# Weight blocks of half the size, more buffers of half the size, and conditioning products eight at a time

## The chip, the cores and the metric

The kernel runs on one core of a Trainium2 chip. The metric is the time of one execution on the device, in microseconds (us), as the median of three runs. A profiled execution is taken beside them.

## The reference, cut to what matters

It is one inference step of a two-layer decoder trunk, all in float32, for 256 prompt tokens and 8 sequences of 4 new tokens each (288 columns of work in all).

```python
cond = silu(c)
for layer in range(2):
    mod = cond @ w_ada[layer] + b_ada[layer]            # (2048) x (2048, 12288)
    sh1, sc1, g1, sh2, sc2, g2 = split(mod, 6)
    h = rms(x, g_mix[layer]) * (1 + sc1) + sh1
    y = mixer(h)            # layer 0: GLA + gated DeltaNet; layer 1: SSD + S5
    x = x + g1 * y
    h = rms(x, g_ffn[layer]) * (1 + sc2) + sh2
    up = causal_dwconv(h @ w_up[layer])                 # (2048) x (2048, 11264)
    a, g = split(up, 2)
    x = x + g2 * ((silu(g) * a) @ w_down[layer])        # (5632) x (5632, 2048)
y = rms(x, g_final)
```

Each mixer has an input projection (`w_in_ab`, `w_in_cd`), recurrences in chunks with many small products, and an output projection.

## The kernel before, in words

**Weights and products.** Every large matrix goes through `weights` (line 170): a block of 4 tiles of 128 input rows by 256 output columns is loaded from HBM by SyncE's DMA queue into a buffer `raw` (512 KB, pool `wraw`, 5 buffers), ScalarE rounds it to `whi` (line 179), VectorE takes the remainder `wlo = raw - whi` (line 180), both into pool `whl` (3 buffers each), and TensorE makes 24 products of 288 columns with it (lines 206 to 208 in `project`, 235 to 237 in `project_parts`, which runs the first projection): high times high, high times low, low times high, for each of 4 tiles and 2 halves of the columns.

**Conditioning.** The modulation vectors `mod` of both layers need 12 matrices of 2048 by 2048 that are used once, with 9 columns of data padded to 32. Here the weight is what streams: `ada_groups` (line 1912) makes four products of 512 columns with a stationary `cond` of 32 columns, one on each quarter of the array's columns. `ada_quarter` (line 1945) does the first two matrices in pieces at the start; `ada_steps` (line 1918) does the ten later ones as background work: it loads one tile of 128 rows in two DMAs of 512 KB, makes its four products, and so on 16 times. These loads (`araw`) share the 5 buffers of `wraw`.

**Pace.** `weights` calls `c.step()` (line 57) for each block; a step advances the generators that `c.background` has registered, one `yield` each so many steps. The tables of S5 and the conditioning for layer 1 run so behind the first feed-forward.

**Order.** The program is written in one sequence; a scheduler then sets the order on each engine by priority (program order) and by its own estimate of what is ready, and gives out the buffers. Each engine runs its order strictly. A product may so be moved between others, but a queue never overtakes itself. Waits are by semaphores; the loads of SyncE and ScalarE share eight of them (`DMAHW0` to `DMAHW7`), and a load waits until the earlier one on its semaphore has landed.

**Small loads.** `rows_in` (line 447) brings convolution states in through a `raw` buffer, `RB` = 6 columns of tiles at a time; `load_consts` (line 670) brings in constants in pieces of 1024 columns. `small_proj` (line 1970) uses the same pools.

**Stages by time in the profile.** 0 to 246 us: start, conditioning of the first mixer, `project_parts`. 246 to 984 us: first mixer and its output projection. 984 to 1804 us: feed-forward of layer 0. 1804 to 2460 us: second mixer. 2460 to 3279 us: feed-forward of layer 1, with conditioning in its first part only.

Of the kernel before, what the change touches and what calls it, by code (L numbers as in the profile page):

```python
# [9 lines left out]
F32 = mybir.dt.float32  # L10
# [5 lines left out]
P = 128  # L16
# [3 lines left out]
T = SEQ + NS * DS  # L20
TS = T + NS + 2
D = 2048
KT = D // P
FF = 5632
EPS = 1e-6
RB = 6
# [15 lines left out]


class Ctx:
    raw_bufs, hl_bufs, kb = 5, 3, 4
    count = 0

    def __init__(self):
# [170 lines left out]
def project_parts(c, w, cols, act, part, tick, ready):  # L219


    nc = c.nc
    for q in range(KT // 4):
        for i, (c0, out, scale) in enumerate(cols):
            tick(q, i)
            if i == part and q + 1 < KT // 4:
                ready(q + 1)
            hi, lo = weights(c, w, 4 * q, 4, c0, 2 * P)
            ps = c.pp.tile([P, 2, 512], F32, tag="pp", name="pp")
            for j in range(2):  # L230
                js = slice(j * P, (j + 1) * P)
                for k in range(4):
                    ah, al = act(4 * q + k)
                    o = ps[:, j, :T]
                    nc.tensor.matmul(o, hi[:, k, js], ah, start=(k == 0), stop=False)  # L235
                    nc.tensor.matmul(o, hi[:, k, js], al, start=False, stop=False)  # L236
                    nc.tensor.matmul(o, lo[:, k, js], ah, start=False, stop=(k == 3))  # L237
            if q == 0:
                nc.scalar.activation(out, ps[:, :, :T], AF.Copy, scale=scale)
            else:  # L240
                nc.vector.scalar_tensor_tensor(out, ps[:, :, :T], scale, out, ALU.mult, ALU.add)
# [202 lines left out]
    return [(st[i * rows:(i + 1) * rows], d[i]) for i in range(q)]  # L444


def rows_in(c, o, src, rows, nt, q, stage=None, RB=RB):

    nc = c.nc
    m = nt // q  # L450
    ov = o.rearrange("p (c q) r -> p c (q r)", q=q)
    w = q * rows
    g = 512 // w
    stage = stage or (lambda: c.wraw.tile([P, RB * P], F32, tag="raw", name="rowst"))
    parts = []
    for s0 in range(0, m, RB):
        sn = min(RB, m - s0)
        st = stage()[:, :RB * P].rearrange("p (c n) -> p c n", n=P)
        parts.append((s0, sn, st))
        for a, b in row_parts(st[:w, :sn], src, s0, sn, rows, q):  # L460
            nc.gpsimd.dma_start(a, b)

    def place():
        for s0, sn, st in parts:
            for c0 in range(0, sn, g):
                n = min(g, sn - c0)
                ps = mtile(c)
                for j in range(n):
                    transpose(c, ps[:, j * w:(j + 1) * w], st[:w, c0 + j, :])
                nc.scalar.copy(ov[:, s0 + c0:s0 + c0 + n, :], ps[:, :n * w].rearrange("p (c w) -> p c w", w=w))  # L470

    return place
# [197 lines left out]
def load_consts(c, cf, cm):  # L670
    nc = c.nc
    c.seg = c.const.tile([P, 13, P], F32R, name="seg")
    m8 = c.const.tile([P, NCM], mybir.dt.uint8, name="cm8")
    for dst, src, n in ((c.seg.rearrange("p l t -> p (l t)"), cf, 13 * P), (m8, cm, NCM)):
        for o in range(0, n, 1024):
            m = min(1024, n - o)
            st = c.wraw.tile([P, 1024], F32, tag="raw", name="craw")
            nc.sync.dma_start(st[:, :m], src[:, o:o + m])
            nc.vector.tensor_copy(dst[:, o:o + m], st[:, :m])
    c.pre, c.suf = c.seg[:, 7, :].bitcast(F32), c.seg[:, 8, :].bitcast(F32)  # L680
    c.segs = c.seg[:, 9:13, :]
    c.pres, c.sufs = c.seg[:, 11, :].bitcast(F32), c.seg[:, 12, :].bitcast(F32)
    c.sel = c.const.tile([P, 64], F32R, name="sel")
    nc.vector.tensor_copy(c.sel, c.cf[:, NS + 35:NS + 99])
    c.mk = m8[:, :8 * P].rearrange("p (l t) -> p l t", t=P)
    c.mkT = m8[:, 8 * P:15 * P].rearrange("p (l t) -> p l t", t=P)
# [1225 lines left out]
def ada_groups(c, ps, cond, pieces, ks, first, last):  # L1912

    for r in range(4):
        c.nc.tensor.matmul(ps[32 * r:32 * r + 32, :], cond[:, ks[r], :], pieces[r], start=first, stop=last)  # L1915


def ada_steps(c, cond, w, which, bias, mod):

    nc = c.nc  # L1920
    ps = c.pa.tile([P, 512], F32, tag="pa", name="pa")
    for k in range(KT):
        pieces = []
        for h in range(2):
            raw = c.wraw.tile([P, 1024], F32, tag="raw", name="araw")
            nc.sync.dma_start(raw, w[k * P:(k + 1) * P, which * D + h * 1024:which * D + (h + 1) * 1024])
            pieces += [raw[:, 0:512], raw[:, 512:1024]]
            if h:
                ada_groups(c, ps, cond, pieces, [k] * 4, k == 0, k == KT - 1)
            yield  # L1930
    pt = mtile(c)
    for t in range(0, 4, 2):
        sb = c.misc.tile([P, T], F32, tag="tmp", name="adas", bufs=2)[:, :2 * P]
        nc.scalar.copy(sb, ps[:, t * P:(t + 2) * P])
        for j in range(2):
            transpose(c, pt[:, (t + j) * P:(t + j + 1) * P], sb[:, j * P:(j + 1) * P])
    pv = pt.rearrange("p (t j s) -> p j t s", t=4, j=4)
    mv = mod.rearrange("p (j t) s -> p j t s", t=4)
    bv = bias.rearrange("p (j t) -> p j t", t=4)
    for t in range(4):  # L1940
        nc.vector.tensor_tensor(mv[:, :, t], pv[:, :, t, 0:9], bc(bv[:, :, t], 2, 9), ALU.add)
    yield


def ada_quarter(c, cond, w, which, q, bias, mod):

    nc = c.nc
    ps = c.pa.tile([P, 512], F32, tag="pa", name="pa")
    c0 = which * D + q * 512
    for k in range(0, KT, 4):  # L1950
        pieces = []
        for k0 in (k, k + 2):
            raw = c.wraw.tile([P, 2, 512], F32, tag="raw", name="araw")
            nc.sync.dma_start(raw, w[k0 * P:(k0 + 2) * P, c0:c0 + 512].rearrange("(k p) n -> p k n", p=P))
            pieces += [raw[:, 0], raw[:, 1]]
            if k0 > k:
                ada_groups(c, ps, cond, pieces, range(k, k + 4), k == 0, k == KT - 4)
            yield
# [303 lines left out]
def trunk(tc, I, O):  # L2262
    nc = tc.nc
    with ExitStack() as ctx:
# [107 lines left out]
        fso = lambda l: O["ffn_conv_s"][l].rearrange("s j n -> (s j) n")  # L2372
        with tc.tile_pool(name="s5prep", bufs=1, reuse_waits="tile") as tp:
            c.background(1.9, *[ada(l, i) for l, i in ((0, 5), (1, 1), (1, 0), (1, 2))])
            c.background(2, s5_tables(c, tp, I["s5_A_re"][0], I["s5_A_im"][0], I["s5_log_dt"][0],
                                      (I["s5_B_re"][0], I["s5_B_im"][0]), (I["s5_C_re"][0], I["s5_C_im"][0]), s5d))
            c.pace(math.inf)
            c.pace(1.5, 48)
            ss1, h1 = SumSquares(c, x), norm("g_mix1", 1, 1, 0)
            ffn(c, 0, x, h, ss, mods[0][:, 5], pr, I["w_ffn_up"][0], I["w_ffn_down"][0], fst(0), O["ffn_conv_p"][0, 0], fso(0),  # L2380
                done(ss1, h1))
            c.finish()
# [75 lines left out]
```

## Time and profile before

| | us |
|---|---|
| median of 3 runs | 3285.08 |
| lowest and highest | 3272.85, 3291.9 |
| profiled execution, its own time | 3281.18 |
| its span from first to last instruction | 3279.2 |
| granted TensorE clock, mean | 0.99 |
| TensorE (PE) busy | 3178.5 (97%) |
| VectorE (DVE), ScalarE (ACT) busy | 2074.9 (63%), 1456.5 (44%) |
| moved by DMA | 663.82 MB, mean 202 GB/s |

Products on PE overlap: one is shown as some 0.3 us long, while the next starts 0.13 us after it. So a full PE is read from how many products start in a stretch and from the distance of their starts, not from the busy share. PEld are the weight loads of PE. A conditioning product stands in the trace as two records. A line is that of the kernel's file before, unless it is said otherwise.

### The profile page before, as it was taken

Reading aid. Unit: us, or ns where it says so; the run is one execution under the profiler, and the core shown is the slowest. Engines: PE = TensorE matmul, PEld = TensorE weight load, DVE = VectorE, ACT = ScalarE, POOL = GpSimd, SP = SyncE. Lnnn points to the kernel's source line nnn. Section 1 sums busy time; section 2 is a strip of 40 time slices with the busy share of each in tenths; the row PEclk is TensorE's granted clock in tenths of the full one; section 3 lists DMA queues with packets and bytes.
Section 4 is the critical chain, followed back from the end, with each engine's and each line's share of the span. In section 5 each row is a group of like instructions: output and inputs, shape, how many; then the busy total and the mean of one; then the engine's idle time right before and its main releaser. Section 6 shows DMA issues by size and latency. Waiting matters only on the chain.

```text
span 3279.2 us, 58982 instructions
## 1 busy us (share of the span) xinstructions
PE 3178.5 (97%) x23220; PEld 2839.6 (87%) x23220; DVE 2074.9 (63%) x4303; ACT 1456.5 (44%) x2286; POOL 430.4 (13%) x792
## 2 busy tenths in 40 slices
PE   7999999999999999999999999999999999999998
PEld 3678777888989999999999977877989999999997
DVE  3346756666787566667665776667775556565566
ACT  2333333343554434343444675444464435444353
POOL 2010011111231100010101210112131001010020
PEclk9999999999999999999999999999999999999999
DMA  8876675455667777778777665764467755555553
GB/s 292 264 224 193 200 253 154 152 172 173 184 208 233 225 234 242 236 239 254 234 242 233 201 199 169 242 211 158 150 198 229 226 167 167 163 165 168 166 172 108
DMA packets 506617, 663.82 MB, mean 202 GB/s; under 512 B 42409, under 2 KB 436454, under 8 KB 506330
## 3 DMA queue, kind: packets, MB, share of 16 engines
q1 hardware_dynamic: 470930, 610.68, 58.8%
q0 software_dynamic: 14272, 40.76, 4.1%
q10 hardware_dynamic: 21136, 8.61, 1.0%
q8 instruction: 183, 3.00, 0.4%
q14 instruction: 96, 0.78, 0.1%
HBM read 634.13 MB, written 25.79 MB: 201 GB/s over the span
## 4 chain that ended last, share of the span: by engine, by line
PE 83%; DMA 8%; ACT 3%; DVE 3%; issue 2%; POOL 0%; SPq 0%; ACTq 0%; DVEq 0%; POOLq 0%
PE pp L206 22%; PE pp L208 21%; PE pp L207 21%; PE pa L1915 6%; DMA raw<-in_w_in_ab 2%; DMA raw<-in_w_in_cd 2%; PE pm L121 1%; DMA araw<-in_w_ada 1%; DVE wlo L180 1%; ACT whi L179 1%; PE pp L237 1%; PE pp L235 1%; PE pm L1125 1%; PE pp L236 1%; PE pm L1121 1%
## 5 line engine op out<-in xcount | busy, mean ns | idle before, releaser
L180 DVE TENSOR_TENSOR wlo<-raw,whi 128x1024 fp32r<-128x1024 f32 x768 | 944.4, 1231 | 736.4 <-ACT whi L179 725.0
L179 ACT CAST whi<-raw 128x1024 fp32r<-128x1024 f32 x768 | 805.4, 1049 | 1278.9 <-PE pp L207 671.4
L206 PE MATMUL pp<-hhi,whi 128*128 128x288 f32 (+1 forms) x4480 | 1347.9, 301 | 3.2 <-ACT whi L179 1.9
L208 PE MATMUL pp<-hhi,wlo 128*128 128x288 f32 (+1 forms) x4480 | 1339.1, 299 | 6.8 <-DVE wlo L180 6.6
L207 PE MATMUL pp<-hlo,whi 128*128 128x288 f32 (+1 forms) x4480 | 1336.2, 298 | 0.1
L206 PEld LDWEIGHTS pp<-hhi,whi 128*128 128x128 f32 x4480 | 848.9, 190 | 121.2 <-issue 81.5
L208 PEld LDWEIGHTS pp<-hhi,wlo 128*128 128x128 f32 x4480 | 848.5, 189 | 23.6 <-DVE wlo L180 11.3
L207 PEld LDWEIGHTS pp<-hlo,whi 128*128 128x128 f32 x4480 | 848.4, 189 | 11.0 <-issue 9.8
L206 PE MATMUL pp<-hh,whi 128*128 128x288 f32 x1408 | 417.3, 296 | 0.0
L208 PE MATMUL pp<-hh,wlo 128*128 128x288 f32 x1408 | 416.6, 296 | 0.0
L207 PE MATMUL pp<-hl,whi 128*128 128x288 f32 x1408 | 413.5, 294 | 0.0
L1915 PE MATMUL pa<-araw,cond 128*32 128x512 f32 x1536 | 265.8, 606 | 12.5 <-DMA araw<-in_w_ada 12.2
L206 PEld LDWEIGHTS pp<-hh,whi 128*128 128x128 f32 x1408 | 264.7, 188 | 15.1 <-issue 13.4
L207 PEld LDWEIGHTS pp<-hl,whi 128*128 128x128 f32 x1408 | 266.6, 189 | 0.0
L208 PEld LDWEIGHTS pp<-hh,wlo 128*128 128x128 f32 x1408 | 264.2, 188 | 0.1
L532 DVE SCALAR_TENSOR_TENSOR cv<-pad,params,cv 128x304 f32<-128x304 f32 (+1 forms) x460 | 224.8, 533 | 20.3 <-ACT cv L530 12.0
L525 POOL COPY ffnpo<-pad 128x4 f32<-128x4 f32 x88 | 66.9, 761 | 1223.0 <-ACT pad L522 1223.0
L431 DVE SCALAR_TENSOR_TENSOR x<-pp,mod,x 128x256 f32<-128x256 f32 x256 | 112.4, 479 | 76.7 <-PE pp L208 75.8
L530 ACT ACTIVATE cv<-pad,params 128x304 f32<-128x304 f32 (+1 forms) x212 | 125.3, 637 | 8.9 <-ACT pad L523 1.1
L1915 PEld LDWEIGHTS pa<-araw,cond 128*32 128x32 f32 x1536 | 39.3, 108 | 63.5 <-issue 35.4
L235 PE MATMUL pp<-hhi,whi 128*128 128x288 f32 x256 | 79.0, 309 | 6.3 <-ACT whi L179 6.2
L521 POOL COPY pad<-ffnsi 128x32 f32<-128x32 f32 x88 | 82.3, 935 | 16.9 <-ACT ffnsi L470 16.9
(797 smaller groups left out, 3008.6 us busy)
## 6 DMA issues: line engine op xcount, KB each, us to landing
araw<-in_w_ada SPq DMA_DIRECT2D x384, 512.0 KB, 4.7
raw<-in_w_ffn_up SPq DMA_DIRECT2D x352, 512.0 KB, 3.8
raw<-in_w_ffn_down SPq DMA_DIRECT2D x176, 512.0 KB, 3.5
raw<-in_w_in_ab SPq DMA_DIRECT2D x112, 512.0 KB, 5.1
raw<-in_w_in_cd SPq DMA_DIRECT2D x56, 512.0 KB, 5.1
raw<-in_w_out_ab SPq DMA_DIRECT2D x32, 512.0 KB, 5.7
raw<-in_w_out_cd SPq DMA_DIRECT2D x32, 512.0 KB, 3.4
s5d<-5p_D ACTq DMA_DIRECT2D x8, 838.0 KB, 5.7
```

The costliest lines, as they stand in the source:

```text
L179: nc.scalar.copy(hi[:, :n], raw[:, :n])
L180: nc.vector.tensor_tensor(lo[:, :n], raw[:, :n], hi[:, :n].bitcast(F32), ALU.subtract)
L206: nc.tensor.matmul(o, hi[:, k, js], ah, start=(k0 + k == first), stop=False)
L207: nc.tensor.matmul(o, hi[:, k, js], al, start=False, stop=False)
L208: nc.tensor.matmul(o, lo[:, k, js], ah, start=False, stop=(k0 + k == last))
L235: nc.tensor.matmul(o, hi[:, k, js], ah, start=(k == 0), stop=False)
L431: nc.vector.scalar_tensor_tensor(x[:, k + j, :SEQ], y[:, j, :SEQ], g[:, k + j, 8:9], x[:, k + j, :SEQ], ALU.mult, ALU.add)
L521: nc.gpsimd.tensor_copy(pv[:, :, :, 0:n], sv)
L525: nc.gpsimd.tensor_copy(po[:, :, t0:t0 + 2], pad[:, :, SEQ:SEQ + n].rearrange("p j r -> p r j"))
L530: nc.scalar.activation(a, pad[:, j, 0:L], AF.Identity, scale=w(0), bias=pr(bname, t0 + j))
L532: nc.vector.scalar_tensor_tensor(a, pad[:, j, i:i + L], w(i), a, ALU.mult, ALU.add)
L1915: c.nc.tensor.matmul(ps[32 * r:32 * r + 32, :], cond[:, ks[r], :], pieces[r], start=first, stop=last)
```

## The change

A block has 2 tiles of input rows in place of 4 (256 KB), so all that `weights` does is done twice as often at half the size. The pool `wraw` has 12 buffers of 256 KB in place of 5 of 512 KB, and `whl` 5 of half the size in place of 3. `ada_steps` lets seven steps pass, then loads two tiles of rows in eight DMAs of 256 KB and makes eight products. The rates of background work are halved where they count steps, except those of conditioning, which now has twice as many yields for the same work.

```diff
-    raw_bufs, hl_bufs, kb = 5, 3, 4
+    raw_bufs, hl_bufs, kb = 12, 5, 2
...
@@ project_parts
-            hi, lo = weights(c, w, 4 * q, 4, c0, 2 * P)
             ps = c.pp.tile([P, 2, 512], F32, tag="pp", name="pp")
-            for j in range(2):
-                js = slice(j * P, (j + 1) * P)
-                for k in range(4):
-                    ah, al = act(4 * q + k)
...
+            for k0 in range(0, 4, 2):
+                hi, lo = weights(c, w, 4 * q + k0, 2, c0, 2 * P)
+                for j in range(2):
+                    js = slice(j * P, (j + 1) * P)
+                    for k in range(2):
+                        ah, al = act(4 * q + k0 + k)
...
-def rows_in(c, o, src, rows, nt, q, stage=None, RB=RB):
+def rows_in(c, o, src, rows, nt, q, stage=None, RB=4):
...
@@ load_consts
-        for o in range(0, n, 1024):
-            m = min(1024, n - o)
-            st = c.wraw.tile([P, 1024], F32, tag="raw", name="craw")
+        for o in range(0, n, 512):
+            m = min(512, n - o)
+            st = c.wraw.tile([P, 512], F32, tag="raw", name="craw")
...
@@ ada_steps
-    for k in range(KT):
+    for k0 in range(0, KT, 2):
+        for _ in range(7):
+            yield
         pieces = []
-        for h in range(2):
-            raw = c.wraw.tile([P, 1024], F32, tag="raw", name="araw")
-            nc.sync.dma_start(raw, w[k * P:(k + 1) * P, which * D + h * 1024:which * D + (h + 1) * 1024])
-            pieces += [raw[:, 0:512], raw[:, 512:1024]]
-            if h:
-                ada_groups(c, ps, cond, pieces, [k] * 4, k == 0, k == KT - 1)
-            yield
+        for k in (k0, k0 + 1):
+            for n in range(which * D, (which + 1) * D, 512):
+                pieces.append(c.wraw.tile([P, 512], F32, tag="raw", name="araw"))
+                nc.sync.dma_start(pieces[-1], w[k * P:(k + 1) * P, n:n + 512])
+        for k in (k0, k0 + 1):
+            ada_groups(c, ps, cond, pieces[4 * (k - k0):4 * (k - k0) + 4], [k] * 4, k == 0, k == KT - 1)
+        yield
...
@@ ada_quarter
-            raw = c.wraw.tile([P, 2, 512], F32, tag="raw", name="araw")
-            nc.sync.dma_start(raw, w[k0 * P:(k0 + 2) * P, c0:c0 + 512].rearrange("(k p) n -> p k n", p=P))
-            pieces += [raw[:, 0], raw[:, 1]]
+            for i in range(2):
+                pieces.append(c.wraw.tile([P, 512], F32, tag="raw", name="araw"))
+                nc.sync.dma_start(pieces[-1], w[(k0 + i) * P:(k0 + i + 1) * P, c0:c0 + 512])
...
-            c.background(2, s5_tables(c, tp, I["s5_A_re"][0], I["s5_A_im"][0], I["s5_log_dt"][0],
+            c.background(4, s5_tables(c, tp, I["s5_A_re"][0], I["s5_A_im"][0], I["s5_log_dt"][0],
...
-            c.pace(1.5, 48)
+            c.pace(3, 96)
```

How the order moves shows best at three places. In the changed file the line of the conditioning product is 1916 and that of its load 1930; lines after those have moved by one to three.

PE in the feed-forward of layer 0 (`hh`, `hl` are the activations, `pa` the result of the conditioning), before:

```order
L206 MATMUL pp<-hh,whi 128x288
L207 MATMUL pp<-hl,whi 128x288
L208 MATMUL pp<-hh,wlo 128x288
L1915 MATMUL pa<-araw,cond 32x512 x4
L206 MATMUL pp<-hh,whi 128x288
L207 MATMUL pp<-hl,whi 128x288
```

and now:

```order
L206 MATMUL pp<-hh,whi 128x288
L207 MATMUL pp<-hl,whi 128x288
L208 MATMUL pp<-hh,wlo 128x288
L1916 MATMUL pa<-araw,cond 32x512 x8
L206 MATMUL pp<-hh,whi 128x288
L207 MATMUL pp<-hl,whi 128x288
```

Four conditioning products stood between weight products every 72 or 96 of these; now eight stand together about every 180.

PE in the first mixer, beside the inverse of the DeltaNet (`d_b`, `d_V`), before:

```order
L207 MATMUL pp<-hlo,whi 128x288
L208 MATMUL pp<-hhi,wlo 128x288
L1915 MATMUL pa<-araw,cond 32x512
L1121 MATMUL pm<-d_b,d_V 128x128 x4
L1915 MATMUL pa<-araw,cond 32x512 x3
L206 MATMUL pp<-hhi,whi 128x288
L207 MATMUL pp<-hlo,whi 128x288
```

and, a little further on, now:

```order
L207 MATMUL pp<-hlo,whi 128x288
L208 MATMUL pp<-hhi,wlo 128x288
L1916 MATMUL pa<-araw,cond 32x512 x8
L206 MATMUL pp<-hhi,whi 128x288
L207 MATMUL pp<-hlo,whi 128x288
```

Before, four products were often cut in two by others; now most stand eight together there too.

SyncE's load queue in the feed-forward of layer 0, with what each load waits for, before:

```order
L1926 DMA araw_14173<-in_w_ada 128x1024 [waits DMAHW7_49,DVE_49]
L175 DMA raw_14175<-in_w_ffn_up 128x4x256 [waits DMAHW4_49,DMAHW1_49,DVE_49]
L175 DMA raw_14211<-in_w_ffn_up 128x4x256 [waits DMAHW5_49,DMAHW2_49,DVE_49]
L1926 DMA araw_14241<-in_w_ada 128x1024 [waits PE_49]
L175 DMA raw_14260<-in_w_ffn_up 128x4x256 [waits DMAHW0_49,PE_49]
```

and now:

```order
L175 DMA raw_16308<-in_w_ffn_up 128x2x256 [waits DMAHW0_49,DVE_49]
L1930 DMA araw_16326<-in_w_ada 128x512 [waits DMAHW1_49,DVE_49]
L1930 DMA araw_16328<-in_w_ada 128x512 [waits DMAHW2_49,DVE_49]
L1930 DMA araw_16330<-in_w_ada 128x512 [waits DMAHW3_49,DVE_49]
L1930 DMA araw_16332<-in_w_ada 128x512 [waits DMAHW4_49,DVE_49]
L1930 DMA araw_16334<-in_w_ada 128x512 [waits DMAHW5_49,DVE_49]
L1930 DMA araw_16336<-in_w_ada 128x512 [waits DMAHW6_49,DVE_49]
L1930 DMA araw_16338<-in_w_ada 128x512 [waits DMAHW7_49,DVE_49]
L1930 DMA araw_16340<-in_w_ada 128x512 [waits DMAHW0_49,DVE_49]
L175 DMA raw_16350<-in_w_ffn_up 128x2x256 [waits DMAHW1_49,DVE_49]
```

Conditioning loads came singly between weight loads; now eight come in a row, and the eight semaphores are taken in turn, so that at most eight loads are under way.

## Rows read from the trace of the kernel before

**Rows 1.** the page, part 4: shares of the chain that ended last.

```profile
PE 83%; DMA 8%; ACT 3%; DVE 3%; issue 2%; POOL 0%; SPq 0%; ACTq 0%; DVEq 0%; POOLq 0%
PE pp L206 22%; PE pp L208 21%; PE pp L207 21%; PE pa L1915 6%; DMA raw<-in_w_in_ab 2%; DMA raw<-in_w_in_cd 2%; PE pm L121 1%; DMA araw<-in_w_ada 1%; DVE wlo L180 1%; ACT whi L179 1%; PE pp L237 1%; PE pp L235 1%; PE pm L1125 1%; PE pp L236 1%; PE pm L1121 1%
```

**Rows 2.** busy time by stretch: stretch, us, PE, PEld, DVE, ACT, POOL, PEclk, DMA share, GB/s.

```profile
0.00:246.00 246.00, 212.58 (x1297) 148.21 (x1298) 102.52 (x160) 69.35 (x104) 34.86 (x67) 0.97 0.82 260
246.00:984.00 738.00, 712.02 (x5172) 601.16 (x5171) 498.69 (x1161) 305.56 (x518) 111.43 (x187) 0.98 0.59 187
984.00:1804.00 820.00, 819.57 (x6115) 759.01 (x6114) 538.82 (x1239) 351.30 (x476) 81.17 (x174) 1.00 0.76 237
1886.00:2460.00 574.00, 551.13 (x4035) 466.23 (x4028) 399.00 (x884) 309.13 (x614) 103.13 (x179) 0.99 0.60 190
2624.00:3116.00 492.00, 492.00 (x3707) 492.00 (x3706) 282.89 (x403) 216.95 (x269) 44.32 (x90) 1.00 0.53 166
```

**Rows 3.** timeline of PE near 1108 us: start, us, engine, line, operation.

```profile
1108.19 0.29 PE L208 MATMUL pp<-hhi,wlo 128*128 128x288 f32 x1
1108.42 1.06 PE L1915 MATMUL pa<-araw,cond 128*32 128x512 f32 x8
1109.41 0.40 PE L206 MATMUL pp<-hhi,whi 128*128 128x288 f32 x1
1109.65 0.30 PE L207 MATMUL pp<-hlo,whi 128*128 128x288 f32 x1
```

**Rows 4.** timeline of PE near 144 us and near 608 us.

```profile
144.75 1.99 PE L1915 MATMUL pa<-araw,cond 128*32 128x512 f32 x16
...
607.10 1.04 PE L1915 MATMUL pa<-araw,cond 128*32 128x512 f32 x2
608.07 1.16 PE L1121 MATMUL pm<-d_b,d_V 128*128 128x128 f32 x8
609.16 1.06 PE L1915 MATMUL pa<-araw,cond 128*32 128x512 f32 x6
```

**Rows 5.** groups by form: line, engine, operation, count | busy us, mean ns | idle before.

```profile
L180 DVE TENSOR_TENSOR wlo<-raw,whi 128x1024 fp32r<-128x1024 f32 x768 | 944.4, 1231 | 736.4 <-ACT whi L179 725.0 <-PE pm L121 5.5 <-PE pp L208 4.5
L179 ACT CAST whi<-raw 128x1024 fp32r<-128x1024 f32 x768 | 805.4, 1049 | 1278.9 <-PE pp L207 671.4 <-DMA raw<-in_w_ffn_up 177.0 <-DMA raw<-in_w_in_ab 163.5
L247 DVE TENSOR_TENSOR hl<-nf,hh 128x576 fp32r<-128x576 f32 x44 | 33.2, 756 | 19.3 <-ACT hh L246 19.3
L246 ACT CAST hh<-nf 128x576 fp32r<-128x576 f32 x44 | 29.6, 674 | 47.1 <-DVE nf L584 46.9
```

**Rows 6.** the chain by line, of 246 to 984 us and of 1886 to 2460 us.

```profile
by line: PE pp L206 13.5%; PE pp L207 12.8%; PE pp L208 12.8%; DMA raw<-in_w_in_ab 7.0%; PE pa L1915 6.6%; issue 3.9%; PE pm L1125 3.5%; PE pm L1121 3.4%; DMA gs_S<-in_state_gla 2.7%; PE pm L1129 2.4%; DVE wlo L180 2.2%; PE pm L121 1.9%; PE
...
by line: PE pp L208 13.8%; PE pp L206 13.6%; PE pp L207 13.5%; DMA raw<-in_w_in_cd 8.8%; PE pa L1915 5.5%; DVE wlo L180 2.9%; issue 2.8%; PE pm L121 2.7%; ACT whi L179 2.5%; ACT cd_y L1836 2.3%; PE s_py L1493 2.3%; PE pm L1852 2.2%; DMA s_S
```

**Rows 7.** pieces of the chain: start, us, what.

```profile
224.59 1.92 POOL rowst L461 x3
...
317.04 5.82 DMA raw<-in_w_in_ab
322.96 1.06 ACT whi L179
324.04 1.24 DVE wlo L180
```

**Rows 8.** DMA issues: tile, queue, count, KB each, median us to landing.

```profile
raw<-in_w_ffn_up SPq DMA_DIRECT2D x352, 512.0 KB, 3.8
raw<-in_w_in_ab SPq DMA_DIRECT2D x112, 512.0 KB, 5.1
s_S<-in_state_ssd POOLq DMA_DIRECT2D x16, 256.0 KB, 4.3
```

**Rows 9.** busy time of line 179 by stretch: stretch, us, ACT, PEclk, DMA share, GB/s.

```profile
246.00:984.00 738.00, 132.90 (x127) 0.98 0.59 187
1886.00:2460.00 574.00, 115.12 (x110) 0.99 0.60 190
```

More of the change, by code (lines that the diff above doesn't have):

```diff
@@ L227, in project_parts @@
                 ready(q + 1)
-            hi, lo = weights(c, w, 4 * q, 4, c0, 2 * P)
             ps = c.pp.tile([P, 2, 512], F32, tag="pp", name="pp")
-            for j in range(2):
-                js = slice(j * P, (j + 1) * P)
-                for k in range(4):
-                    ah, al = act(4 * q + k)
[L234 to L237, printed above, removed]
+            for k0 in range(0, 4, 2):
[4 more added lines that the diff above has]
+                        ah, al = act(4 * q + k0 + k)
+                        o = ps[:, j, :T]
+                        nc.tensor.matmul(o, hi[:, k, js], ah, start=(k0 + k == 0), stop=False)
+                        nc.tensor.matmul(o, hi[:, k, js], al, start=False, stop=False)
+                        nc.tensor.matmul(o, lo[:, k, js], ah, start=False, stop=(k0 + k == 3))
             if q == 0:
```

## The prediction

> **What bounds the kernel now.** I read the shares of the chain first: 83% of it is work of PE, 8% loads, 3% each ACT and DVE [rows 1]. Then the stretches, because that share is a mean over stages of two kinds [rows 2]. From 2624 to 3116 us PE starts 3707 products in 492 us, one each 0.133 us, across the border of a block every 24 products: nothing but the array limits it there, and halving a block costs PE nothing by itself. From 984 to 1804 us it is nearly as full (6115, a tenth of them conditioning records). From 246 to 984 and from 1886 to 2460 us, the two mixers, it starts 7.0 a microsecond in place of 7.5, many of them small: it waits on chains through ACT, DVE and loads. The first 246 us have 5.3 a microsecond, with the loads 82% busy at 260 GB/s. So three things of the change can count: what conditioning costs PE, how fast a block gets from HBM to PE in the mixers and at the start, and the extra work of ACT and DVE.
>
> **Switching to conditioning and back.** The last weight product before a group of four starts at 1108.19, the second after it at 1109.65 [rows 3]. Without the group that would be two distances, 0.27; so a group costs 1.46 - 0.27 = 1.19 us of PE. Eight products in a row were busy for 1.99 us where four take 1.06 [rows 3, 4]: the second four add 0.93, and a merge saves 0.26 us. A group cut in two pays in full twice: two records and six records took 1.04 and 1.06 us around a small product [rows 4]; put together they save 1.19. Counted along the order, the number of runs of conditioning products, and of fours in them (a run of five to eight is two):
>
> - start: 45 runs, 54 fours before; 33 and 49 now
> - first mixer: 68 and 68; 43 and 61
> - feed-forward 0: 59 and 59; 30 and 60
> - second mixer: 51 and 52; 32 and 44
> - feed-forward 1: 12 and 12; 6 and 12
>
> At 1.19 us for a run and 0.93 for each further four that is 7.8, 13.0, 6.6, 12.4 and 1.6 us less work of PE. In the feed-forwards I count all of it. In the mixers the lines of PE that are shown make up 57% and 54% of the chain [rows 6], over the whole run PE has 83% [rows 1]; I take three quarters, so 9.8 and 9.3; at the start, where loads and PE take turns, half, 3.9. Together **-31 us**; the bounds are -8 (the feed-forwards alone) and -41 (all of it).
>
> **A block's way from HBM to PE.** In the mixers the chain often goes load, ACT, DVE: 5.82, 1.06 and 1.24 us for one block [rows 7]. What is one 512-column instruction? Between 576 columns (674 ns on ACT, 756 on DVE) and 1024 (1049 and 1231) a column costs 0.84 and 1.06 ns [rows 5], so 512 columns take about 620 and 688 ns. The chain holds 7.0% of 738 us = 52 us of weight loads in the first mixer and 8.8% of 574 = 51 in the second; DVE's split has 2.2% and 2.9%, 16 and 17 us; ACT's has 2.5%, 14 us, in the second [rows 6], and I take as much for the first. The casts then give back 0.43/1.06 of 28 us = 11 and 0.55/1.24 of 33 = 15. For the load no row shows this very size from this queue. The nearest 256 KB load took 4.3 us on POOL's queue beside 5.1 for 512 KB of weights [rows 8], a gain of 16% or 16 us; the other end is zero, if eight loads under way share the same bandwidth. I take the middle, 8. If all these links stayed where they are, 34 us would go. But a chain that is shortened in one place is soon replaced by the next, so I take half, **-17 us**, with bounds 0 and -42.
>
> On this the Trainium skill speaks against the change: "DMA: Bandwidth & Descriptors", section Bandwidth, asks to batch a DMA to 1 MiB or more, and its section on the anatomy of a DMA gives, for the queue of GpSimd, a fixed 2.0 us plus the bytes at 436 GB/s. By that a load goes from 3.2 to 2.6 us (estimates), and twice as many would cost 60% more if they ran one after another. The trace does not agree that they do: 512 KB in 3.8 us [rows 8] is 138 GB/s for one load alone, while the feed-forward moves 237 GB/s [rows 2]. They overlap, so the sum does not change by this rule.
>
> **More casts.** Two halves cost 2 x 620 - 1049 = 190 ns more on ACT, and 2 x 688 - 1231 = 145 on DVE. In the feed-forwards that is hidden: there DVE is busy 66% and ACT 43% of the time [rows 2], and the extra is 0.15 to 0.2 us for each block's 24 x 0.133 = 3.2 us. In the mixers 127 + 110 blocks are split [rows 9]: 45 us of ACT and 34 of DVE. DVE is busy 68 to 70% there and ACT 41 to 54% [rows 2], and both stand on a small part of the chain; I let 15% through, **+12 us**, bounds 0 and +79. That casts of half the length make others in ACT's queue wait less for them works the other way and is in this share.
>
> **Small things.** The state of the first convolution now takes two more DMAs from POOL; three of its issues took 1.92 us on the chain [rows 7], so **+1 us**. SyncE issues twice as many loads; it mostly waits for buffers, so nothing, as long as buffers are ahead. The background rates stay the same: half the steps, twice the size. Twelve buffers and five splits of half the size are, in whole blocks, 6 + 2.5 in place of 5 + 3.
>
> Sum: -31 - 17 + 12 + 1 = -35 us against the profiled execution's 3281, so about 3246; the median shown is 4 us above that execution. I forecast **3246 us**, its own range 3225 to 3268. What a measurement can tell from no change is 0.5%, 16 us.
>
> **Rivals.**
>
> *Links shorten in full.* If the mixers and the start are bound by the block's way, with buffers that come free in smaller pieces, the -42 and the -41 both come and the casts cost nothing: 3281 - 83 + 1 = 3199. For it: the chain enters load links one after another from 317 us on [rows 7]. Against: PE works during most of them.
>
> *Only the feed-forwards pay.* The mixers' chains swallow the merges, and shorter links and more casts cancel: 3281 - 8 = 3273, no change that can be told. For it: PE waits for small products there, not for time on the array.
>
> *Slower: the casts stand in the mixers' way.* The 79 us of ACT and DVE work lie on the chains of the two mixers, as each small step queues behind one more fixed part. Only DVE's part: 3281 + 34 - 8 = 3307; both: 3352. It decides if the chain of the mixers then shows DVE and ACT with well over the present few per cent. Against: DVE idles 30% there, and the scheduler can put a small step between two halves.
>
> *Slower: bursts starve PE.* Eight conditioning loads take 8 of 12 buffers until their products are made. Left are 4 loaded and 5 split half blocks, 9 x 1.6 = 14 us of work; a load lands in about 5 [rows 8]. It decides if the eight land more than 14 us after the first was issued. At 1 us for each of the 65 runs of eight, 3246 + 65 = 3311. Of the same kind is the limit of eight loads under way: 2.1 MB in place of up to 2.6. At the start's 260 GB/s [rows 2] that decides only if a half load takes over 8.1 us.
>
> **How the numbers follow.** The forecast gets 0.51, full links 0.17, the feed-forwards alone 0.18, casts 0.09, bursts 0.05. Faster by over 0.5%: 0.51 + 0.17 + 0.02 of the third case = 0.70; within it 0.16; slower 0.14. The range of eight in ten takes in the first three cases, 3190 to 3300.
>
> **What would show it.** Right: in the feed-forward of layer 0, conditioning rows of x16 of about 1.95 us, and the stage some 7 us shorter; casts of 620 and 690 ns; the mixers together 20 to 30 us shorter, with load links on the chain of well under 5 us. Wrong: the half load landing no sooner than the whole one, ACT or DVE with twice their share of the mixers' chain, or PE waiting for loads of weights in the feed-forwards.

## The result and the profile after

| | us |
|---|---|
| after: median of 4 runs | 3226.4 (3224.88 to 3228.87) |
| before: median of 4 runs, same chip | 3281.26 (3272.85 to 3291.9) |
| ratio, 95% interval | 0.9825 (0.9808 to 0.9842) |
| profiled execution after, its span | 3228.87, 3227.1 |

The change takes 55 us off by the medians, 1.75% by the ratio; forecast were 35 (3246, own range 3225 to 3268, the range of eight in ten 3190 to 3300). The page of the changed kernel, shares of the chain that ended last:

```profile
PE 87%; DMA 5%; DVE 4%; ACT 2%; issue 2%; POOL 0%; SPq 0%; DVEq 0%; ACTq 0%; POOLq 0%
```

Against [rows 1] the loads' share went from 8% to 5%, PE's from 83% to 87%. The casts and the conditioning product in the groups of the same page:

```profile
L179 ACT CAST whi<-raw 128x512 fp32r<-128x512 f32 x1536 | 946.8, 620 | 1192.5 <-PE pp L207 963.2
L180 DVE TENSOR_TENSOR wlo<-raw,whi 128x512 fp32r<-128x512 f32 x1536 | 1060.1, 700 | 621.8 <-ACT whi L179 600.2
...
L1916 PE MATMUL pa<-araw,cond 128*32 128x512 f32 x1536 | 238.2, 605 | 5.3 <-DMA araw<-in_w_ada 5.1
```

The casts last 620 and 700 ns, forecast were 620 and 688 from [rows 5]. Its DMA issues (tile, queue, count, KB each, median us to landing):

```profile
araw<-in_w_ada SPq DMA_DIRECT2D x768, 256.0 KB, 5.0
raw<-in_w_ffn_up SPq DMA_DIRECT2D x704, 256.0 KB, 3.1
...
raw<-in_w_in_ab SPq DMA_DIRECT2D x224, 256.0 KB, 4.5
raw<-in_w_in_cd SPq DMA_DIRECT2D x112, 256.0 KB, 3.7
```

Half a block lands 0.6 to 0.7 us earlier than a whole one [rows 8].

For the comparison by place I cut both traces at the same work: at the last product of `project_parts`, and where the product that adds up the squares for each later norm starts (line 304; 305 after). Before, stretch by stretch (us, PE, PEld, DVE, ACT, POOL, PEclk, DMA share, GB/s):

```profile
0.00:220.20 220.20, 192.31 (x1196) 132.80 (x1197) 88.79 (x143) 60.47 (x88) 27.93 (x60) 0.98 0.83 267
220.20:921.20 701.00, 674.73 (x4896) 567.70 (x4895) 465.02 (x1057) 276.20 (x471) 95.78 (x164) 0.98 0.59 186
921.20:1857.90 936.70, 931.02 (x6895) 860.79 (x6893) 623.83 (x1450) 422.98 (x595) 117.55 (x212) 1.00 0.74 231
1857.90:2390.00 532.10, 507.76 (x3735) 427.98 (x3734) 372.58 (x858) 284.13 (x578) 85.84 (x154) 0.99 0.60 191
2390.00:3265.50 875.50, 871.25 (x6502) 848.95 (x6501) 519.77 (x783) 410.57 (x552) 103.34 (x203) 1.00 0.57 175
```

And after:

```profile
0.00:199.30 199.30, 184.44 (x1196) 130.26 (x1197) 93.63 (x178) 65.66 (x121) 30.42 (x62) 1.00 0.91 295
199.30:887.40 688.10, 662.62 (x4895) 569.84 (x4895) 477.85 (x1175) 295.82 (x586) 88.08 (x166) 0.98 0.60 191
887.40:1812.20 924.80, 921.07 (x6897) 864.48 (x6895) 652.95 (x1712) 469.15 (x859) 119.60 (x212) 1.00 0.73 235
1812.20:2338.80 526.60, 503.41 (x3732) 434.27 (x3732) 384.75 (x955) 299.00 (x675) 84.75 (x157) 0.97 0.61 193
2338.80:3213.70 874.90, 869.76 (x6502) 849.99 (x6501) 546.53 (x1042) 454.77 (x812) 109.07 (x201) 1.00 0.57 175
```

PE's records are the same in number within three in each pair, so the lengths compare: start -20.9 us, first mixer -12.9, feed-forward 0 -11.9, second mixer -5.5, feed-forward 1 -0.6, and -0.3 behind the last norm. At the start the same bytes move at 295 GB/s in place of 267.

### The profile page after: what moved, and what is told of

It reads as the page before. It is cut to its first block, busy times and chain, and to the rows that moved or that the text cites. A ratio compares the mean times of both kernels' runs of the same rounds, so it can differ in the third digit from the quotient of the medians.

```text
span 3227.1 us, 64199 instructions
## 1 busy us (share of the span) xinstructions
PE 3142.7 (97%) x23220; PEld 2850.2 (88%) x23220; DVE 2160.6 (67%) x5075; ACT 1586.6 (49%) x3054; POOL 431.9 (13%) x794
## 4 chain that ended last, share of the span: by engine, by line
PE 87%; DMA 5%; DVE 4%; ACT 2%; issue 2%; POOL 0%; SPq 0%; DVEq 0%; ACTq 0%; POOLq 0%
PE pp L206 23%; PE pp L208 23%; PE pp L207 23%; PE pa L1916 6%; DMA raw<-in_w_in_ab 2%; PE pm L121 2%; DVE wlo L180 1%; PE pp L238 1%; PE pp L236 1%; DMA araw<-in_w_ada 1%; PE pp L237 1%; PE pm L1126 1%; PE pm L1122 1%; DMA gs_S<-in_state_gla 1%; DMA s_S<-in_state_ssd 1%
## 5 line engine op out<-in xcount | busy, mean ns | idle before, releaser
L179 ACT CAST whi<-raw 128x512 fp32r<-128x512 f32 x1536 | 946.8, 620 | 1192.5 <-PE pp L207 963.2
L180 DVE TENSOR_TENSOR wlo<-raw,whi 128x512 fp32r<-128x512 f32 x1536 | 1060.1, 700 | 621.8 <-ACT whi L179 600.2
L1916 PE MATMUL pa<-araw,cond 128*32 128x512 f32 x1536 | 238.2, 605 | 5.3 <-DMA araw<-in_w_ada 5.1
L526 POOL COPY ffnpo<-pad 128x4 f32<-128x4 f32 x88 | 21.4, 243 | 1153.9 <-ACT pad L523 1153.9
L522 POOL COPY pad<-ffnsi 128x32 f32<-128x32 f32 x88 | 138.4, 1573 | 15.5 <-ACT ffnsi L471 15.5
L238 PE MATMUL pp<-hhi,wlo 128*128 128x288 f32 x256 | 76.8, 300 | 2.0 <-DVE wlo L180 1.9
```

The costliest lines, as they stand in the source:

```text
L179: nc.scalar.copy(hi[:, :n], raw[:, :n])
L180: nc.vector.tensor_tensor(lo[:, :n], raw[:, :n], hi[:, :n].bitcast(F32), ALU.subtract)
L238: nc.tensor.matmul(o, lo[:, k, js], ah, start=False, stop=(k0 + k == 3))
L522: nc.gpsimd.tensor_copy(pv[:, :, :, 0:n], sv)
```

## The experiments

Each time below is the median of 4 to 12 executions, and each ratio is against the kernel before, timed beside it. The same cut of every profile, in us ("12/5" is the number of load and split buffers):

| kernel | start | mixer 1 | ffn 0 | mixer 2 | ffn 1 |
|---|---|---|---|---|---|
| before, 5/3 whole | 220.2 | 701.1 | 936.7 | 532.0 | 875.5 |
| after, 12/5 | 199.3 | 688.2 | 924.8 | 526.5 | 874.9 |
| e1_fours, 12/5 | 199.6 | 681.7 | 937.1 | 528.7 | 875.4 |
| e2_ten_six, 10/6 | 209.2 | 682.4 | 939.3 | 525.6 | 874.4 |
| e3_before_eight, 5/3 whole | 217.2 | 702.1 | 950.6 | 527.6 | 875.8 |
| e4_fourteen_four, 14/4 | 197.4 | 667.2 | 928.2 | 520.1 | 874.9 |
| f1_sixteen_three, 16/3 | 198.4 | 673.8 | 943.5 | 544.3 | 879.8 |
| f2_casts_twice, 12/5 | 204.3 | 689.4 | 923.3 | 527.0 | 877.0 |
| f3_loads_twice, 12/5 | 207.0 | 695.7 | 926.0 | 530.1 | 873.7 |
| f4_before_seven_two, 7/2 whole | 208.6 | 691.5 | 949.0 | 534.9 | 880.9 |
| g1_fourteen_fours, 14/4 | 198.0 | 677.8 | 937.0 | 521.0 | 878.8 |
| g2_fourteen_mix, 14/4 | 197.3 | 678.4 | 927.8 | 519.3 | 875.6 |
| g3_twelve_mix, 12/5 | 199.6 | 685.7 | 924.8 | 521.6 | 875.6 |

Each row is one profile. Stretches with the same code differ by up to 0.7 us at the start (g1 and g2), 4 us in the first mixer (e1 and g3) and 5 us in the second (after and g3), so only larger differences are read there. The granted clock differs as well: in the first mixer it is 0.98 before, after and in e2, and 0.99 in e1, e4, g1, g2 and g3. One hundredth of 690 us is 7 us of full-speed time, so a part of the differences there is time at the lower of the clock's two levels; whether that is a cause or follows from waits of PE is shown for one place only, below.

**e1_fours: the change with conditioning four at a time.**

```diff
-    for k0 in range(0, KT, 2):
-        for _ in range(7):
+    for k in range(KT):
+        for _ in range(3):
             yield
...
```

> The change with one part undone: the later conditioning products are made four at a time (one tile of rows, four loads of 256 KB, three empty steps), all buffers and blocks as in the change. Theory (merges are worth 0.26 us each on a full PE): feed-forward of layer 0 goes from 811 to 819 us, that of layer 1 loses 1.6 us, the mixers lose 4 to 12 us; about 3240, between 3236 and 3248. Rival (the merge is nothing, all of the gain is finer blocks): 3226 within 5 us. Rival (the merge is the main part of the gain): over 3255.

Measured: 3237.33 us (3232.54 to 3240.1), ratio 0.9838 (0.9816 to 0.9859), within the interval of the change. But the places differ: feed-forward 0 loses all of its gain (937.1, before 936.7), and the first mixer, expected to lose, is 6.5 us shorter than with eights (g3 below, with fours there too, 2.5). So eights pay in the feed-forward, and with 12 buffers not in the first mixer.

**e3_before_eight: before, with eight at a time.** The loads stay at 512 KB, so a burst takes 4 of the 5 buffers.

```diff
-    for k in range(KT):
+    for k0 in range(0, KT, 2):
+        for _ in range(3):
+            yield
         pieces = []
-        for h in range(2):
...
+        for k in (k0, k0 + 1):
+            for h in range(2):
...
```

> The kernel before with one part of the change done alone: later conditioning products eight at a time, from four loads of 512 KB in the five full-size buffers. Theory: merges save 0.26 us each in the feed-forwards as in the change (feed-forward of layer 0 some 8 us shorter than 820), but four of five buffers are then held by conditioning, so weight blocks arrive late in the mixers and eat it up: 3281 within 20 us, the start unchanged near 220 us. Rival (merging is all that counts): 3255 or less. Rival (a burst starves PE wherever it stands): feed-forward of layer 0 longer than 820 us, total over 3310.

Measured: 3290.0 us, ratio 1.0004 (0.9991 to 1.0017): nothing. Feed-forward 0 became 14 us longer; that is a miss. PE's waits in that stretch (total us, times, longest):

```profile
PE pp L208 <- DVE wlo L180: 10.5, 15, 1.3
PE pp L206 <- ACT whi L179: 8.5, 9, 2.6
```

In that stretch of the changed kernel neither of these waits appears. With 5 large buffers a burst of eight starves PE. Small pieces alone are not enough: with ten small buffers, the same bytes, the stage is 939.3 us (e2, next), as long as with fours and 12 (e1, 937.1). Eights paid there with 12 and 14 small buffers; eights with seven large ones were not tried.

**e2_ten_six and e4_fourteen_four: the same bytes of SBUF, divided otherwise.**

```diff
-    raw_bufs, hl_bufs, kb = 12, 5, 2
+    raw_bufs, hl_bufs, kb = 10, 6, 2
```

```diff
-    raw_bufs, hl_bufs, kb = 12, 5, 2
+    raw_bufs, hl_bufs, kb = 14, 4, 2
```

> The change with 10 load and 6 split buffers of half the size, which is to the byte what stood there before (5 and 3 of full size). Theory (the gain at the start comes from finer pieces: a buffer is free, loaded and split after half the data): the first projection still ends near 199 us, within 5 us; total 3226 within 10 us. Rival (the gain at the start comes from 20% more load buffers): it ends 10 us or more later, near 210 to 215 us, total 3238 or more.

> The change with 14 load and 4 split buffers (the same bytes in all as the change). Theory (finer pieces matter, the share of bytes between the two pools little): start near 199 us within 5 us, total 3226 within 10 us. Rival (more load buffers make the start): start 5 us or more shorter. Rival (split blocks ahead of PE carry the mixers): mixers 10 us or more longer, total 3240 or more.

Measured: 10/6 3246.28 us, ratio 0.9864 (0.9842 to 0.9886), as its rival said; 14/4 **3202.37 us** (3201.33 to 3206.29), ratio 0.9737 (0.9716 to 0.9758), faster than both kernels and 14 us below the lowest that was expected. Ten small buffers hold as many bytes as five large ones, and with them the start takes 209.2 us: of its 20.9, 11 come with the smaller pieces (and with the few merges there, which the run holds too) and 10 with bytes ahead. With ten, feed-forward 0 is 14 us longer than with twelve. With 14, the first mixer gains another 21, at a granted clock of 0.99 in place of 0.98.

**f1_sixteen_three: further the same way** (16, 3).

> The change with 16 load and 3 split buffers (again the same bytes). Theory (loads ahead are what the start and the first mixer lack; 12 to 14 gave 25 us): the first mixer a few us shorter than with 14, but three split half blocks are 4.8 us of PE's work against 0.62 + 0.70 us of casts and what queues before them, so the feed-forwards may begin to wait: 3202 within 12 us. Rival (split blocks ahead are not needed at all): 3190 or less. Rival (they are needed as soon as they are few): over 3226, with weight products waiting on lines 179 and 180 in the mixers.

Measured: 3251.94 us, ratio 0.9901 (0.9882 to 0.9921). PE's waits over the whole span:

```profile
PE pa L1916 <- DMA araw<-in_w_ada: 12.4, 7, 4.6
PE pp L208 <- DVE wlo L180: 11.2, 17, 1.6
```

That is the slow rival's total (over 3226). With three split buffers PE waits for VectorE's split (11.2 us; 1.9 in the first 199 us of the changed kernel and 0.7 on line 208 later), but these waits are 11 of the 50 us lost against 14/4. The second mixer, 24 us longer, has 0.2 us of them, 5.8 of waits for conditioning loads (1.8 with 14/4) and a granted clock of 0.96 against 0.98; why it is so much longer stays open. 14/4 is the best of these four.

**f2_casts_twice: every cast and split in two halves of 256 columns.**

```diff
-    nc.scalar.copy(hi[:, :n], raw[:, :n])
-    nc.vector.tensor_tensor(lo[:, :n], raw[:, :n], hi[:, :n].bitcast(F32), ALU.subtract)
+    for o in range(0, n, n // 2):
+        s = slice(o, o + n // 2)
+        nc.scalar.copy(hi[:, s], raw[:, s])
+        nc.vector.tensor_tensor(lo[:, s], raw[:, s], hi[:, s].bitcast(F32), ALU.subtract)
```

> The change with each cast of 512 columns made as two of 256, on ACT and on DVE; loads, buffers and products as in the change. Each split adds the fixed part once more, some 0.19 us on ACT and 0.17 on DVE (two halves of the change against one cast of before, by its trace), for 474 half blocks in the mixers: 90 and 80 us of extra work there. Theory of the prediction (15% comes through): +25 us, 3250. Rival (casts stand on the mixers' chains): +80 to +170. Rival (they are hidden): within 8 us of 3226.

Measured: 3233.37 us, ratio 0.9837 (0.9815 to 0.986). Its casts, by form:

```profile
L182 DVE TENSOR_TENSOR wlo<-raw,whi 128x256 fp32r<-128x256 f32 x3072 | 1193.7, 427 | 601.5 <-ACT whi L181 580.1 <-PE pp L209 4.8 <-PE pa L1918 2.0
L181 ACT CAST whi<-raw 128x256 fp32r<-128x256 f32 x3072 | 1101.0, 404 | 1114.2 <-PE pp L209 818.6 <-ACT whi L181 96.5 <-DMA raw<-in_w_in_ab 74.3
```

ACT worked 154 us longer on casts and DVE 134, and the kernel took about 4 us more by the ratios, whose intervals overlap. In the profile 5 of 7 us stand at the start, where the granted clock was 0.98 in place of 1.00; both mixers stayed within 1.2 us. The casts are hidden, and the rival by which they stand in the mixers' way falls.

**f3_loads_twice: each half block in two loads of 128 KB.**

```diff
-    nc.sync.dma_start(raw[:, :n].rearrange("p (k n) -> p k n", k=kn),
-                      w[k0 * P:(k0 + kn) * P, c0:c0 + cn].rearrange("(k p) n -> p k n", p=P))
+    for k in range(kn):
+        nc.sync.dma_start(raw[:, k * cn:(k + 1) * cn], w[(k0 + k) * P:(k0 + k + 1) * P, c0:c0 + cn])
```

> The change with each weight block loaded in two DMAs of 128 KB in place of one of 256; casts, buffers and products as in the change. At most eight loads are under way, so now 1.0 MB of weights in place of 2.1, and each costs its fixed part again. Theory (the load queue has room in the feed-forwards, not where many blocks are fetched at once): feed-forwards within 5 us, start and first mixer 10 to 40 us longer, total 3240 to 3270. Rival (the size of a load does not matter): within 8 us of 3226. Rival (fixed parts add up): feed-forward of layer 0 longer by 20 us or more, total over 3300.

Measured: 3245.78 us, ratio 0.9879 (0.9858 to 0.9901): 8 us longer at the start and 7.5 in the first mixer, 1.2 in feed-forward 0, within what was expected. Here it counts that loads are large; whether by the limit of eight under way or by SyncE's issues, this run doesn't separate. Part of the start's 8 us may be the clock: the granted clock was 0.95 there, 1.00 in the changed kernel.

**f4_before_seven_two: before, its conditioning in fours as it was, with 7/2 buffers of the old size.**

```diff
-    raw_bufs, hl_bufs, kb = 5, 3, 4
+    raw_bufs, hl_bufs, kb = 7, 2, 4
```

> The kernel before, blocks of full size, with 7 load and 2 split buffers in place of 5 and 3 (the same bytes). Theory (loads ahead help the start and the first mixer whatever the block, but two split blocks of full size leave PE 3.2 us for casts of 2.3 us and the work queued before them): start 8 us or more shorter, feed-forwards longer by 10 to 80 us; total between 3260 and 3340. Rival (only the number of load buffers counts, the size of the block nothing): 3250 or less, near the change. Rival (load buffers do nothing without smaller blocks): start within 4 us of 220.

Measured: 3283.12 us, ratio 0.9991 (0.9977 to 1.0004). Against before the start is 11.6 us shorter and the first mixer 9.6, and feed-forward 0 is 12 longer, the second mixer 3 and feed-forward 1 5. More bytes ahead help at the start with large blocks too; what is lost there with two large split buffers takes it back. In the same bytes, only small blocks allow both more loads ahead and enough splits.

**g1, g2, g3: where a burst costs.** g1 is 14/4 with fours everywhere, g2 14/4 with fours in the first mixer alone, g3 the change with fours there alone.

```diff
...
-    for k0 in range(0, KT, 2):
-        for _ in range(7):
+    for k0 in range(0, KT, rows):
+        for _ in range(4 * rows - 1):
             yield
...
-                c.background(1, ada(0, 2), ada(0, 4), ada(0, 3))
+                c.background(1, ada(0, 2, 1), ada(0, 4, 1), ada(0, 3, 1))
```

> 14 load and 4 split buffers with the conditioning of the background in fours instead of eights. If a burst of eight costs time only because it takes 8 of 12 buffers, then with 14 the eights are the better choice everywhere, as their merged runs save PE work: the fours should take longer by the feed-forward merges (9 to 10 us) and by some of the first mixer and the second, 3212 to 3225 us against 3202 with eights. Rival: a burst of eight still costs as much in the mixers with 14 buffers, and the gain of 14 buffers is of another kind (more bytes ahead): then the two differ as with 12 buffers, fours in all 10 us longer by the feed-forwards, 5 to 13 us shorter in the first mixer, 3195 to 3212 us. The first mixer's stage separates them: 667 us with eights; longer with fours by the first theory, 655 to 662 by the rival.

> 14 load and 4 split buffers, eights everywhere except in the first mixer, where the conditioning runs in fours. By the theory that 14 buffers hold a burst of eight without harm: first mixer not shorter than 667 us, longer by up to 9 us for the merges lost, 3202 to 3212 us in all. By the rival (the burst costs there with any number of buffers): first mixer 655 to 662 us, 3190 to 3198 us.

> The change itself, with fours in place of eights in the first mixer alone. Theory: with 12 buffers the burst of eight costs some 13 us just after the first projection, which merged runs later in that mixer give back in part; fours there give a first mixer of about 682 us as in the run with fours everywhere (688 with eights), while feed-forward 0 keeps the eights' gain: 3226 - 7 = 3219 us, 3214 to 3223. Rival: what the run with fours gained there is chance of the order and does not carry over: 688 us and 3226 to 3235 us.

Measured: g1 3227.24 us, ratio 0.9818 (0.9805 to 0.9831); g2 3213.34, 0.9776 (0.9762 to 0.979); g3 3222.99, 0.9809 (0.9795 to 0.9822). g1 and g2 lie 2 and 1 us above the ends of their ranges, with the first mixer at 677.8 and 678.4: with 14 buffers eights save 11 us there, and the rival (655 to 662) falls. Feed-forward 0 gains 9.2 by eights (g1 against g2). g3 is inside its range; its interval and that of the change overlap, so for the change itself the net of bursts in the first mixer is small. It is two large sums, as the time for the same weight products (`pp`), counted in their order, shows:

| weight products | after (12, eights) | g3 (12, fours) | g2 (14, fours) | e4 (14, eights) |
|---|---|---|---|---|
| 769 to 1500 | 178.9 | 168.1 | 165.6 | 163.2 |
| 1501 to 3000 | 404.5 | 413.7 | 405.4 | 398.1 |

In the first stretch eights cost 10.8 us with 12 buffers and save 2.4 with 14; in the second they save 9.2 and 7.3. Runs with the same code differ by 2 us here (e1 has 166.3 and 411.7 beside g3's 168.1 and 413.7). f2 and f3, which also have 12 buffers and eights, repeat the first stretch: 178.9 and 179.0.

**One burst in the changed kernel.** Where the 10.8 us stand can be read in the trace between 292 and 320 us. SyncE's queue (start, us, engine, line):

```profile
292.76 4.17 SPq L1930 DMA_DIRECT2D araw<-in_w_ada  x8
298.03 11.81 SPq L175 DMA_DIRECT2D raw<-in_w_in_ab  x5
```

ACT, with its idle time and what ended it:

```profile
301.13 0.62 ACT L179 CAST whi<-raw 128x512 fp32r<-128x512 f32 x1 [0.98 <-DMA araw<-in_w_ada]
308.10 0.62 ACT L179 CAST whi<-raw 128x512 fp32r<-128x512 f32 x1 [6.35 <-DMA raw<-in_w_in_ab]
308.62 0.40 ACT L1057 CAST ho_B<-ho_r 2x256 fp32r<-2x256 f32 x1
```

PE:

```profile
304.11 0.29 PE L208 MATMUL pp<-hhi,wlo 128*128 128x288 f32 x1
304.25 0.29 PE L206 MATMUL pp<-hhi,whi 128*128 128x288 f32 x1
310.03 0.77 PE L1064 MATMUL pm<-ho_B,sel 64*128 64x256 f32 x2 [5.49 <-DVE ho_B L1058]
...
312.38 0.44 PE L208 MATMUL pp<-hhi,wlo 128*128 128x288 f32 x1
312.62 0.44 PE L206 MATMUL pp<-hhi,whi 128*128 128x288 f32 x1
```

And the stretches around it (columns as above; the 0.50 is PE's granted clock):

```profile
300.00:304.00 4.00, 4.00 (x33) 4.00 (x32) 3.21 (x8) 0.77 (x2) 0.00 (x0) 1.00 1.05 376
304.00:308.00 4.00, 0.54 (x5) 0.30 (x3) 0.00 (x0) 0.00 (x0) 0.00 (x0) 1.00 1.05 344
308.00:312.00 4.00, 1.97 (x5) 1.02 (x5) 2.49 (x6) 1.44 (x3) 0.30 (x1) 0.50 0.41 117
312.00:316.00 4.00, 4.00 (x13) 2.96 (x13) 3.16 (x8) 0.00 (x0) 0.00 (x0) 0.50 0.00 0
316.00:320.00 4.00, 4.00 (x26) 3.98 (x25) 1.15 (x2) 2.68 (x5) 0.00 (x0) 0.72 0.49 129
320.00:324.00 4.00, 4.00 (x33) 2.40 (x32) 3.66 (x2) 1.41 (x3) 0.00 (x0) 1.00 0.13 22
```

Eight conditioning loads go out, three state loads of 512 KB follow on POOL's queue from 296.43 on, and the next block's load goes out only at 298.03, into a full transfer (344 to 376 GB/s); it lands at 308. ACT's queue stands at that block's cast for 6.35 us. Behind it is a cast of 2 by 256 numbers (line 1057) whose input VectorE finished at 303.5; the solver's product on PE needs that, so PE idles for 5.5 us although the numbers for it had been there. From 308, towards the end of the idle time, the granted clock is 0.50, the lower level of 1.2 GHz, until past 316 us: products start 0.24 us apart in place of 0.133. That is some 4 us more (half of the 8 us from 308 and 0.28 of the next 4, less the 1 that falls into the wait). Together 9.5 of the 10.8. f2 and f3 have the same wait (in f2's file the lines are 1066 and 1060), of 300 to 330 us:

```profile
PE pm L1066 <- DVE ho_B L1060: 6.3, 1, 6.3
PE pm L1064 <- DVE ho_B L1058: 6.8, 1, 6.8
```

Neither g3, g2 nor e4 has a wait of PE for line 1058 from 300 to 380 us, and their clock there is 1.00. The late load alone does not make the wait: in e4 and e2 a weight load behind a burst of eight and beside the same state loads took 10 us too (10.2 from 288.5, 9.8 from 315.9), and PE's waits for line 1058 are nothing in e4 and at most 0.3 us each in e2. So it also counts which small step stands behind the cast that waits.

## Why the prediction was right, and where its sizes were off

The direction and the range held; the forecast was 20 us too high, and the measured time lies 1.4 us above the lower end of its own range. The table goes by place, with the two terms for the mixers shared evenly between them (-8.5 and +6 each). The prediction's mixers end at 984 and 2460 us, those of the cut here at 921 and 2390; so the third column counts the runs of conditioning products in both traces at the cut here (45 to 33, 59 to 43, 69 to 34, 41 to 28, 19 to 11; fours in them 54 to 49, 59 to 59, 69 to 66, 42 to 39, 19 to 18), at the prediction's prices and shares:

| place | forecast | the same at this cut | measured |
|---|---|---|---|
| start | -4 | -4 | -20.9 |
| first mixer | -9.8 - 8.5 + 6 + 1 = -11 | -3.1 - 8.5 + 6 + 1 = -4.6 | -12.9 |
| feed-forward 0 | -6.6 | -11.9 | -11.9 |
| second mixer | -9.3 - 8.5 + 6 = -12 | -4.6 - 8.5 + 6 = -7.1 | -5.5 |
| feed-forward 1 | -1.6 | -3.0 | -0.6 |

The prediction's "68 and 68; 43 and 61" of the first mixer is not one stretch in both kernels: at the weight product before which the trace of before has 68 runs in it, the changed kernel's has 48.

**The start was the mis-sized term.** The prediction read "a block's way from HBM to PE" for the mixers alone and gave the start half of its merges. Yet [rows 2] have the loads 82% busy there. The chain of the start by line, before:

```profile
by line: PE pa L1915 15.7%; PE pp L237 13.0%; PE pp L235 12.7%; DMA araw<-in_w_ada 12.6%; PE pp L236 11.7%; DMA raw<-in_w_in_ab 7.8%; DMA xt<-in_x_prompt 4.5%; DMA sraw<-in_w_in_ab 3.8%; PE pm L1964 3.4%; issue 2.7%; ACT whi L179 1.9%; PE p
```

and after:

```profile
by line: PE pa L1916 19.1%; PE pp L238 15.6%; PE pp L236 14.7%; PE pp L237 13.8%; DMA raw<-in_w_in_ab 8.2%; DMA araw<-in_w_ada 6.4%; DMA xt<-in_x_sample 5.2%; PE pm L1967 3.8%; DVE wlo L180 3.6%; issue 1.6%; ACT whi L179 1.2%; ACT adas L196
```

The conditioning loads were 12.6% of 220, 28 us, and are 6.4% of 199, 13 us. The rival of full links named the start, but priced its merges alone, and the step that let it pass is "it mostly waits for buffers, so nothing, as long as buffers are ahead": the number and size of the buffers were the cost. e2 and the change itself give its two halves, 11 us for pieces half the size and 10 for two more of them. f4 gives the second half in the old size: 11.6 for two more large buffers. What the merges at the start gave was not tried.

**Merging in the feed-forward: right.** A burst of eight now costs 2.04 us of PE:

```profile
1074.93 0.29 PE L208 MATMUL pp<-hhi,wlo 128*128 128x288 f32 x1
1075.15 1.92 PE L1916 MATMUL pa<-araw,cond 128*32 128x512 f32 x16
1077.01 0.40 PE L206 MATMUL pp<-hhi,whi 128*128 128x288 f32 x1
1077.24 0.29 PE L207 MATMUL pp<-hlo,whi 128*128 128x288 f32 x1
```

From 1074.93 to 1077.24 are 2.31, less 0.27. Two runs of four cost 2.38 [rows 3], so a merge saves 0.34 us in this place, where 0.26 was taken from [rows 4], busy times. At the prediction's prices the runs counted give 11.9, and 11.9 came; the change against e1 measured 12.3, and g2 against g1 9.2 (67 to 35 runs, 9.3 at those prices).

**The first mixer: 12.9 against 11 is luck.** Of the 11 forecast, 9.8 were merges, and with 12 buffers these did not arrive in sum: with fours (e1, g3) the stage is 19.4 and 15.4 us shorter than before, with eights 12.9. So the other terms, forecast at -1.5 together, gave 15 to 19. f4, with two more large load buffers and one split buffer less, is 9.6 shorter there, e2, with the old bytes in small pieces, 18.7: like the start, this stage gained by its loads more than was priced. Merges are worth their price where the buffers hold: with 14, the runs go from 61 (g1) to 38 (e4), 10.6 us at the prediction's prices, and the stage from 677.8 to 667.2. With 12, from 61 (e1) to 43, the prices give 6.5, and the one burst shown above took 9.5. The last rival is close to that mechanism, but not by its own sign: the last of the eight landed 13.6 us after the first was issued (9.7 after 296.6), its bound was 14, and the block behind them landed after 15. It was priced at 1 us for each of 65 runs; one burst cost 9.5, through ACT's queue and the clock. With 14 buffers that is gone (e4 against g2). With ten the long wait is missing as well (e2), so the number of buffers alone does not explain it; how much a shifted order does was not separated.

**The second mixer: the chain's shares were no saving.** The chain there, by line (1812.2 to 2338.8 us):

```profile
by line: PE pp L206 16.5%; PE pp L208 16.3%; PE pp L207 16.2%; PE pa L1916 4.8%; issue 3.8%; DMA s_S<-in_state_ssd 3.7%; PE pm L121 3.5%; PE s_py L1494 2.4%; PE pm L1853 2.2%; PE pm L1431 1.8%; DMA raw<-in_s_glu_w 1.5%; PE pm L1886 1.4%; PE
```

The loads of `in_w_in_cd`, 8.8% [rows 6], 11.1% of this stage before (59 us), are no longer among the lines shown, so each is under 1.4%, 7 us. Some 50 us of links are gone, and the stage is 5.5 us shorter: PE's weight products took their place, with 49.0% (258 us) in place of 37.8% (201). Weight products 10,601 to 11,200 became 12.2 us shorter, and the next 600 became 6.0 longer. So the links shown on a chain were no measure of the time that goes with them. Merging gave 2.2 us (e1) or 0.9 (g1 against e4), where 4.6 are forecast at this cut; the spread of profiles, 5 us, is larger than what is missing. The clock is a rival: this stage had a granted clock of 0.99 before and 0.97 now, and in the 600 products that became 6.0 us longer (2157.2 to 2330.6 us before, 2098.8 to 2278.3 now) 0.98 and 0.95; g3, with the same code there, had 0.98 and took 4.9 us less. How much the clock took of this stage was not tested.

**Casts: too dear.** Taken was +12. The change made ACT work 141 us longer on casts and DVE 116 (946.8 against 805.4, 1060.1 against 944.4); f2 adds about as much again, 154 and 134, and cost some 4 us (0.12%), which the intervals do not tell from nothing. So the change's own part is of that size or less.

Of the other signs, the mixers became 18.4 us shorter together, not 20 to 30, and the chain still holds single weight loads of 10 us (at 298.03).

On loads the Trainium skill ("DMA: Bandwidth & Descriptors", section Bandwidth) says to batch to 1 MiB or more. The runs agree only below 256 KB: 128 KB cost 0.54% of the time (f3, 0.9879 against 0.9825), while going from 512 to 256 KB at the same buffered bytes made the start 11 us faster (e2).

## What to carry to other kernels

A buffer count times its size is not enough: where a queue waits for free buffers, the same bytes in smaller pieces can feed the loads better (11 us of 220 here). Before bundling small work into bursts, count how many shared buffers a burst holds, what lies behind it in the load queue, and which small step stands behind the cast that waits; then try the neighbouring divisions of the same memory (10/6, 12/5, 14/4, 16/3 gave 0.9864, 0.9825, 0.9737, 0.9901).

## What the runs showed that was not expected

Around one idle stretch of PE of 5.5 us, from 2 us before its end, the granted clock was 0.50 for about 10 us, so the wait cost nearly twice its length. The cost of cutting a cast is small: 1049, 620 and 404 ns on ACT for 1024, 512 and 256 columns, 1231, 700 and 427 on DVE. And a load of 256 KB that usually lands in 4.5 us took 10 behind a burst of eight others, with three state loads of 512 KB from POOL's queue beside them; in e4 as late a load cost PE no wait of that kind.
